# Seven-product down projections in both MLPs of a two-block model, with two pairs of output tiles interleaved

## The chip, the cores and the metric

One core of one Trainium2 chip runs the whole program in one launch. The metric is the device time of an execution in microseconds (us). TensorE multiplies matrices (PE in the profile), VectorE (DVE), ScalarE (ACT) and GpSimd (POOL) do the elementwise work, and DMA queues move data between HBM and the on-chip memory; SP issues most of the weight loads, ACT's queue the rest. Each engine works through its own list of instructions in a fixed order.

## The reference, cut to what matters

Two transformer-like blocks on one sequence of 1024 tokens with 1024 features. Both end in a large MLP with 4096 hidden features, squared ReLU between the two products; block 2 needs modulation vectors from `w_ada`.

```python
x = x + jnp.square(jax.nn.relu(h2 @ w_ff1[l])) @ w_ff2[l]          # block 1
mod = jax.nn.silu(c.astype(jnp.float32)) @ w_ada + b_ada           # [1, 6 * 1024]
mod_c = jax.nn.silu(c_ctx.astype(jnp.float32)) @ w_ada + b_ada
sh1, sc1, gt1, sh2, sc2, gt2 = [m[:, None] for m in jnp.split(mod, 6, axis=-1)]
...
def mlp(s, shift, scale_m):
    hm = rms_norm_2(s, g_norm2) * (1.0 + scale_m) + shift
    return jnp.square(jax.nn.relu(hm @ w_mlp1)) @ w_mlp2           # block 2
x_new = x_new + gt2 * mlp(x_new, sh2, sc2)
```

## The kernel before, in words

Every float32 product is three matmuls of rounded parts: high by high, high by low and low by high (`product`, L123 to L125). `split` (L92, L94) makes the parts: ACT writes the high one, POOL (or DVE on request) subtracts to get the low one. One matmul takes a 128x128 weight and 512 columns. Activations stay on chip as 128x1024 tiles with features on the partitions, in tiles named A, B, C, DD and S by what they hold at the time.

Both MLPs walk through the 4096 hidden features in eight chunks c0 to c7 of 512. A chunk has a first half, the up projection (192 matmuls, `ff1` in block 1), and a second half, the down projection, whose outputs DVE adds to eight running sums of 128x1024.

In block 1 (`mlp1`, L668) the down projection of a chunk is `ff2`: eight calls of `gemm`, 192 matmuls. In chunks 0 to 3 the modulation is woven in: `mod` and `mod_blocks` treat twelve blocks j of 512 columns of `w_ada`, three per chunk. For one block, DVE multiplies eight 128x512 slices of `w_ada` by a column each and adds them up in `acc` (L766, L768, one chain for `c`, and for j below 4 a second for `c_ctx`), transposes the sum (L773) and reduces it (L774); four small matmuls (L778) bring the result to the partitions and DVE adds the bias (L782). The DVE work stands under `later()`, which lets everything else go first. `acc` is one half of the tile DD2 in turn, and the slices come in two loads of 1 MB into DD0 and DD1. Chunk 5 holds `context_norm` and chunk 6 finishes the running sums.

In block 2 (`mlp2`, L1903) the down projection is already done with seven products instead of eight per 2x2 arrangement: `pair_products` takes a pair of output tiles, forms four sums of weight blocks on DVE (tile `ws`, L1849 to L1852), and multiplies them with seven operands that `combine` (L1886 and `put`) forms out of the squared activations: 168 matmuls a chunk. The products gather in four PSUM banks `aux`, and DVE adds each into its outputs (L1970). A bank is used again by a later product only after it has been added out. There are six `aux` buffers and two `acc`.

The order on each engine is set at build time by the framework's scheduler out of program order, priorities (`high_priority`, `later`) and buffers: a tile with one buffer is written again only when all readers of its former content are done.

Of the kernel before, what the change touches and what calls it, by code (L numbers as in the profile page):

```python
# [14 lines left out]
P = 128  # L15
# [39 lines left out]
class Kernel:  # L55
# [319 lines left out]
    def block1(self):  # L375
# [14 lines left out]
        self.delta_setup()  # L390
# [264 lines left out]
    def ff2(self, wap, xh, xl, acc, first, after=None):  # L655
        nc = self.nc

        def evac(ps, js):
            if first:
                nc.scalar.copy(acc[:, js], ps)  # L660
            else:
                nc.vector.tensor_tensor(acc[:, js], ps, acc[:, js], ALU.add)  # L662
            if after:
                after(js)

        self.gemm(wap, xh, xl, evac)

    def mlp1(self):  # L668
# [4 lines left out]
        for c in range(8):  # L673
            ah, al = [], []
            for m in range(4):
                h = self.t(f"C{m}", [P, S], F32R)
                l = self.t(f"C{4 + m}", [P, S], F32R)
                rq = self.t("DD3", [P, 2, S])
                self.ff1(T["w_ff1"][c * 4 + m], self.x1h, self.x1l, h, l, rq[:, 0, :], rq[:, 1, :], rinv if c == 7 else None)
                ah.append(h)  # L680
                al.append(l)
# [7 lines left out]
            for m in range(8 if c < 7 else 0):  # L689
                if c == 0:  # L690
                    acc[m] = self.t(f"S{m}", [P, S])
                after = None
                if c == 6:
                    if m % 2 == 0:
                        x1p = self.t("DD2", [P, 2, S])
                    x1 = x1p[:, m % 2, :]
                    nc.scalar.dma_start(out=x1, in_=self.x1_d[m])

                    def after(js):
                        nc.vector.tensor_tensor(acc[m][:, js], acc[m][:, js], rinv[:, js], ALU.mult)  # L700
# [27 lines left out]
        self.gemm_halves([T["w_ff2"][7, m] for m in range(8)], ah, al, evac)  # L728
# [23 lines left out]
    def mod_blocks(self, j0, j1):  # L752
        nc, T, sil = self.nc, self.T, self.sil
        for j in range(j0, j1):
            n = 2 if j < 4 else 1
            acc = self.t("DD2", [P, 4, 512])[:, 2 * (j % 2) : 2 * (j % 2) + 2]
            for k in range(0, 8, 4):
                w = self.t(f"DD{k // 4}", [P, 4, 512])
                nc.scalar.dma_start(
                    out=w, in_=T["w_ada"][k * P : (k + 4) * P, j * 512 : (j + 1) * 512].rearrange("(a p) c -> p a c", p=P)  # L760
                )
                for kk, i in ((kk, i) for kk in range(4) for i in range(n)):
# [7 lines left out]
            r = w[:, 2, 0 : 16 * n]  # L770
            with self.later():
                for i in range(n):
                    nc.vector.transpose(w[:, i, :], acc[:, i, :])  # L773
                    nc.vector.tensor_reduce(out=r[:, i * 16 : i * 16 + 16], in_=w[:, i, :].rearrange("p (b r) -> p b r", r=32),  # L774
                                            op=ALU.add, axis=AX.X)
# [35 lines left out]
    def delta_setup(self):  # L811
# [14 lines left out]
        self.st = [small(f"st{d}", [P, 8, 64]) for d in range(2)]  # L826
# [266 lines left out]
    def delta_step(self, item, c, el, oacc, seen):  # L1093
# [10 lines left out]
        tmp = self.t(f"dtmp{d}", [64, 4, 64])  # L1104
# [138 lines left out]
    def context_norm(self):  # L1243
# [12 lines left out]
        for k in range(8):  # L1256
            x = raw[:, k, :]
# [6 lines left out]
    def entry(self):  # L1264
# [43 lines left out]
        self.ab = self.t("ab", [P, 8, 32])  # L1308
# [12 lines left out]
    def context(self):  # L1321
# [5 lines left out]
        self.kc2 = [[self.t(f"kc2{p}{i}", [P, L], F32R) for i in range(2)] for p in range(2)]  # L1327
        self.vc = self.t("vc", [P, 2, P])
# [511 lines left out]
    def pair_products(self, raw, ops, evac):  # L1840
# [5 lines left out]
        s = self.t("ws", [P, 4, 2 * P])  # L1846
        a11, a12, a21, a22 = (raw[:, i] for i in range(4))
        s1, s3, s2, s4 = (s[:, i] for i in range(4))
        nc.vector.tensor_tensor(s1, a21, a22, ALU.add)  # L1849
        nc.vector.tensor_tensor(s3, a11, a21, ALU.subtract)  # L1850
        nc.vector.tensor_tensor(s2, s1, a11, ALU.subtract)
        nc.vector.tensor_tensor(s4, a12, s2, ALU.subtract)  # L1852
        banks = {}
        for i, (w, bank, to) in enumerate((
            (a11, 0, [(0, 0)]), (s1, 1, [(1, 1)]), (a12, 2, [(0, 0)]), (s3, 3, [(1, 1)]),
            (s2, 0, [(0, 1), (1, 0), (1, 1)]), (s4, 1, [(0, 1)]), (a22, 3, [(1, 0)]),
        )):
            if i % 2 == 0:
# [15 lines left out]
            for t in to:  # L1874
                evac(t, ps)

    def combine(self, j, qa, qb, ops, m, half):
# [4 lines left out]
        def put(x, i):  # L1882
            h, l = (o[:, j] for o in ops[i])
            self.split(x, h, l)

        sub = lambda o, a, b: nc.vector.tensor_tensor(o, a, b, ALU.subtract)  # L1886
        if m == 0 and half == 0:
            put(qa[:, 0], 0)
        elif m == 0:
            sub(qa[:, 0], qa[:, 1], qa[:, 0])  # L1890
            put(qa[:, 0], 1)
        elif half == 0:
            put(qb[:, 0], 2)
        else:
            sub(qa[:, 1], qb[:, 1], qa[:, 1])
            put(qa[:, 1], 3)
            sub(qa[:, 0], qb[:, 1], qa[:, 0])
            put(qa[:, 0], 4)
            put(qb[:, 1], 5)
            sub(qb[:, 0], qb[:, 0], qa[:, 0])  # L1900
            put(qb[:, 0], 6)

    def mlp2(self):  # L1903
# [3 lines left out]
        for c in range(8):  # L1907
# [3 lines left out]
            qa = [self.t(f"A{6 + j}", [P, 2, 512]) for j in range(2)]  # L1911
            qb = [None, None]
            if c == 0:
                both = self.t("DD3", [P, 2, 2, 512])
                qb = [both[:, j] for j in range(2)]

            def square(m, ps, i):
                if c and m > 1 and i == 0:
                    qb[m % 2] = self.t("S7", [P, 2, 512])
                q = (qa if m < 2 else qb)[m % 2][:, i]  # L1920
                nc.scalar.activation(q, ps, AF.Relu)
                nc.vector.scalar_tensor_tensor(q, ps, 0.0, q, ALU.max, ALU.mult)  # L1922

            if c == 0:
# [216 lines left out]
```

## Time and profile before

| what | value |
|---|---|
| median of 3 runs | 3639.14 us (3637.15 to 3647.19) |
| the profiled execution | 3637.29 us, span 3635.6 us |
| mean granted TensorE clock | 0.978 of full speed |
| PE busy, PEld busy | 3453.7 us (95%), 2777.6 us (76%) |
| DVE busy | 1970.6 us (54%) |
| ACT busy, POOL busy | 1413.0 us (39%), 1627.1 us (45%) |

The span is the time from the first to the last instruction of the profiled execution; 1.7 us lie around it. A single matmul of 512 columns is shown with about 0.4 us, but matmuls are pipelined, and in an undisturbed stretch one starts every 0.23 us. At half clock one starts every 0.43 us.

### The profile page before, as it was taken

What the parts mean: (1) busy time and instruction counts of PE and PEld (TensorE: products, weight loads), DVE (VectorE), ACT (ScalarE), POOL (GpSimd) and SP (SyncE); (2) the same over time, 40 slices, a digit from 0 to 9 for tenths busy, and PEclk for the clock granted to TensorE, in tenths of its full rate; (3) what the DMA queues carried; (4) which work ended last, traced back from release to release, by engine and by line L of the source; (5) the groups of instructions that cost most, each with busy time, mean ns of one, the idle gap of its engine ahead of it and who ended that gap; (6) DMA issues with size and microseconds to landing.
All of it is one profiled execution on the core that took longest, in us unless ns stands there. A gap on an engine that the chain in (4) does not pass through costs nothing. (4 is left out here: it accounts for less than half of the span.)

```text
span 3635.6 us, 49563 instructions
## 1 busy us (share of the span) xinstructions
PE 3453.7 (95%) x17912; PEld 2777.6 (76%) x17912; DVE 1970.6 (54%) x3117; ACT 1413.0 (39%) x3006; POOL 1627.1 (45%) x1894
## 2 busy tenths in 40 slices
PE   8988999999999999999999899979999999999998
PEld 6766777788878887887777788768777877777777
DVE  5576522233454432256377766868876554454445
ACT  4656444423332222225343434334553453333332
POOL 4544422223443333345144475466212565555555
PEclk9998999999999999999999999989999999999999
DMA  3122222243433321133221202211115411111113
GB/s 117 63 70 83 71 67 80 99 139 107 139 115 117 116 70 55 52 100 102 81 76 59 85 33 73 91 56 42 50 48 175 160 57 47 47 47 47 47 47 110
DMA packets 207221, 294.57 MB, mean 81 GB/s; under 512 B 21248, under 2 KB 153472, under 8 KB 206848
## 3 DMA queue, kind: packets, MB, share of 16 engines
q1 hardware_dynamic: 178176, 220.15, 18.4%
q10 hardware_dynamic: 28800, 71.27, 5.9%
q8 instruction: 141, 2.31, 0.3%
q14 instruction: 104, 0.85, 0.1%
HBM read 237.85 MB, written 53.48 MB: 80 GB/s over the span
## 5 line engine op out<-in xcount | busy, mean ns | idle before, releaser
L94 POOL TENSOR_TENSOR wl<-wraw,wh 128x256 fp32r<-128x256 f32 x861 | 717.5, 849 | 1075.6 <-ACT wh L92 1061.5
L124 PE MATMUL acc<-B,wh 128*128 128x512 f32 x1984 | 786.8, 397 | 0.0
L123 PE MATMUL acc<-A,wh 128*128 128x512 f32 (+1 forms) x1920 | 766.6, 399 | 14.4 <-ACT S L1743 11.0
L125 PE MATMUL acc<-A,wl 128*128 128x512 f32 (+1 forms) x1920 | 761.1, 396 | 0.0
L92 ACT ACTIVATE wh<-wraw 128x256 fp32r<-128x256 f32 x925 | 350.4, 411 | 723.2 <-PE acc L124 340.0
L123 PE MATMUL acc<-C,wh 128*128 128x512 f32 x1152 | 456.7, 397 | 4.9 <-DVE S L662 1.5
L125 PE MATMUL acc<-C,wl 128*128 128x512 f32 x1152 | 452.7, 393 | 0.0
L123 PEld LDWEIGHTS acc<-A,wh 128*128 128x128 f32 (+1 forms) x1920 | 361.6, 188 | 105.8 <-ACT S L1743 13.2
L124 PEld LDWEIGHTS acc<-B,wh 128*128 128x128 f32 x1984 | 373.5, 188 | 85.2 <-issue 0.5
L125 PEld LDWEIGHTS acc<-A,wl 128*128 128x128 f32 (+1 forms) x1920 | 361.4, 188 | 85.4 <-POOL wl L94 0.3
L123 PEld LDWEIGHTS acc<-C,wh 128*128 128x128 f32 x1152 | 216.3, 188 | 58.1 <-issue 4.3
L125 PEld LDWEIGHTS acc<-C,wl 128*128 128x128 f32 x1152 | 216.3, 188 | 50.7 <-issue 0.5
L124 PE MATMUL acc<-C,wh 128*128 128x512 f32 x640 | 250.9, 392 | 0.0
L1970 DVE TENSOR_TENSOR DD<-aux,DD 128x512 f32<-128x512 f32 x272 | 178.2, 683 | 64.0 <-PE aux L1873 56.1
L124 PE MATMUL acc<-S,wh 128*128 128x512 f32 x512 | 202.0, 394 | 0.0
L648 DVE SCALAR_TENSOR_TENSOR DD<-acc,DD 128x512 f32<-128x512 f32 x64 | 44.2, 691 | 264.0 <-ACT DD L647 264.0
L94 POOL TENSOR_TENSOR C<-DD,C 128x512 fp32r<-128x512 f32 x64 | 84.4, 1319 | 168.5 <-ACT C L92 168.5
L123 PE MATMUL acc<-DD,wh 128*128 128x512 f32 (+2 forms) x408 | 151.6, 371 | 1.8 <-DVE S L714 1.8
L125 PE MATMUL acc<-DD,wl 128*128 128x512 f32 (+2 forms) x408 | 151.2, 371 | 0.0
L1106 POOL TENSOR_TENSOR dtmp<-st,g_el 64x256 f32<-64x256 f32 x160 | 115.2, 730 | 80.2 <-DVE st L1107 62.7
L124 PEld LDWEIGHTS acc<-C,wh 128*128 128x128 f32 x640 | 120.2, 188 | 25.5
L1872 PE MATMUL aux<-B,wh 128*128 128x512 f32 x256 | 108.3, 423 | 20.0 <-POOL B L94 20.0
(509 smaller groups left out, 6483.8 us busy)
## 6 DMA issues: line engine op xcount, KB each, us to landing
wraw<-in_w_in SPq DMA_DIRECT2D x336, 128.0 KB, 2.1
wraw<-in_w_ff SPq DMA_DIRECT2D x272, 128.0 KB, 2.1
DD<-in_w_ada ACTq DMA_DIRECT2D x24, 1024.0 KB, 5.2
wraw<-in_w_mlp SPq DMA_DIRECT2D x136, 128.0 KB, 2.1
wq<-in_w_mlp SPq DMA_DIRECT2D x32, 512.0 KB, 3.4
wraw<-in_w_out SPq DMA_DIRECT2D x96, 128.0 KB, 2.3
C<-in_rpb SPq DMA_DIRECT2D x24, 384.0 KB, 3.5
tga_d<-S SPq DMA_DIRECT2D x16, 512.0 KB, 3.3
```

The source lines that it names most:

```text
L92: nc.scalar.activation(h, src, AF.Copy)
L94: e.tensor_tensor(l, src, h.bitcast(F32), ALU.subtract)
L123: nc.tensor.matmul(ps, wh, xh, start=first, stop=False)
L124: nc.tensor.matmul(ps, wh, xl, start=False, stop=False)
L125: nc.tensor.matmul(ps, wl, xh, start=False, stop=last)
L648: nc.vector.scalar_tensor_tensor(q[:, js], ps, 0.0, r[:, js], ALU.max, ALU.mult)
L1106: nc.gpsimd.tensor_tensor(tmp, cur[0:64], ev.unsqueeze(2).to_broadcast([64, 4, 64]), ALU.mult)
L1872: nc.tensor.matmul(ps, h, xl[:, k], start=False, stop=False, skip_group_check=not new)
L1970: nc.vector.tensor_tensor(acc[m][:, js], ps, acc[m][:, js], ALU.add)
```

## The change

1. In chunks 0 to 6 of `mlp1` the down projection goes through `pair_products` with seven-product weights; chunk 7 keeps `gemm_halves`. The operands need the tiles C0 to C7 and DD0 to DD2, and the squares DD3.
2. So the modulation moves out of DD0 to DD2: `acc` becomes the single tile `misc`, and the slices of `w_ada` come in four loads of 512 KB in turn into `kc` and `st` (one buffer each). These tiles are used for other things in block 2.
3. `pair_products` takes two pairs at once: three products of the first pair, three of the second, four of the first, four of the second. The sum s1 has a tile `ws1` of its own with two buffers; the other three sums share `ws`, one buffer.
4. `combine` lets DVE make the low parts of operands 4 and 5 instead of POOL.
5. `context_norm` moves from chunk 5 to the seam between the up and down projection of chunk 7, `delta_setup` into block 2, and the block-1 input x1 that chunk 6 adds is loaded into `kc`, `st` and `misc`.

```diff
 def mlp1(self):
-                self.ff1(T["w_ff1"][c * 4 + m], self.x1h, self.x1l, h, l, rq[:, 0, :], rq[:, 1, :], rinv if c == 7 else None)
...
+        for c in range(7):
+            ops = [(self.t(f"C{2 * i}", [P, 2, 512], F32R), self.t(f"C{2 * i + 1}", [P, 2, 512], F32R)) for i in range(4)]
+            for i in range(3):
+                x = self.t(f"DD{i}", [P, 2, 2, 512], F32R)
...
+                for a in range(2):
+                    self.gemm(T["w_ff1"][c * 4 + 2 * a + j], self.x1h, self.x1l, evac)
...
             if c < 4:
                 self.mod(3 * c, 3 * c + 3)
-            if c == 5:
-                self.context_norm()
...
+                    if c == 6:
+                        xs.append(self.t(("kc", "st", "misc")[m % 3], [P, S]))
+                        nc.scalar.dma_start(out=xs[-1], in_=self.x1_d[m])
...
+                    if c == 0 and seen[t] == 1:
+                        nc.scalar.copy(a, ps)
+                    else:
+                        nc.vector.tensor_tensor(a, ps, a, ALU.add)
+                    if c == 6 and seen[t] == (3 if t == (1, 1) else 2):
+                        nc.vector.tensor_tensor(a, a, rinv[:, lat[t[1]]], ALU.mult)
+                        nc.vector.tensor_tensor(a, a, xs[t[0]][:, lat[t[1]]], ALU.add)
...
+            for p in (0, 2):
+                self.pair_products([T["w_ff2"][c, p], T["w_ff2"][c, p + 1]], ops, [adder(p), adder(p + 1)])
...
+        self.context_norm()
...
 def mod_blocks(self, j0, j1):
-            acc = self.t("DD2", [P, 4, 512])[:, 2 * (j % 2) : 2 * (j % 2) + 2]
-            for k in range(0, 8, 4):
-                w = self.t(f"DD{k // 4}", [P, 4, 512])
+            acc = self.t("misc", [P, 2, 512])
+            for k in range(0, 8, 2):
+                w = self.t(("kc", "st")[k // 2 % 2], [P, 2, 512])
...
-            r = w[:, 2, 0 : 16 * n]
+            r = acc[:, 0, 0 : 16 * n]
...
 def pair_products(self, waps, ops, evacs):
+        for n, (p, i) in enumerate([(p, i) for p in range(2) for i in range(3)] + [(p, i) for p in range(2) for i in range(3, 7)]):
+            a11, a12, a21, a22 = (ws[p][:, k] for k in range(4))
+            if i == 0:
+                first[p] = self.t("ws1", [P, 2 * P], bufs=2)
+                nc.vector.tensor_tensor(first[p], a21, a22, ALU.add)
+            s1 = first[p]
+            if i == 3:
+                s = rest[p] = self.t("ws", [P, 3, 2 * P])
+                nc.vector.tensor_tensor(s[:, 2], s1, a11, ALU.subtract)
+                nc.vector.tensor_tensor(s[:, 0], a12, s[:, 2], ALU.subtract)
+                nc.vector.tensor_tensor(s[:, 1], a11, a21, ALU.subtract)
+            s4, s3, s2 = (rest[p][:, k] for k in range(3)) if i >= 3 else (None,) * 3
+            w, bank, to = (
+                (a11, 0, [(0, 0)]), (s1, 1, [(1, 1)]), (a12, 2, [(0, 0)]), (s4, 1, [(0, 1)]), (s3, 3, [(1, 1)]),
+                (s2, 0, [(0, 1), (1, 0), (1, 1)]), (a22, 3, [(1, 0)]),
+            )[i]
...
 def combine(self, j, q, ops, done):
+            put(q[0, 1], 4, "vector")
+            put(q[0, 0], 5, "vector")
```

How the order moves, at three places. First PE in chunk 1 of `mlp1`. Before, the three groups of modulation matmuls (L778) stand apart: one at the end of the up projection and the next some fifty rows into the down projection, here. The names of the rows are output<-activation,weight; C and wh, wl belong to the down projection, DD1 holds the reduced sums.

```order
L124 MATMUL acc_1492_8381<-C7_1457_8165,wh_1487_8357 128x512
L125 MATMUL acc_1492_8381<-C3_1456_8164,wl_1488_8358 128x512
L123 MATMUL acc_1497_8405<-C0_1417_7921,wh_1493_8395 128x512
L778 MATMUL aux_1476_8292<-DD1_1475_8284,id32_1348_7511 32x4 x4
L124 MATMUL acc_1497_8405<-C4_1418_7922,wh_1493_8395 128x512
L125 MATMUL acc_1497_8405<-C0_1417_7921,wl_1494_8396 128x512
```

Now the same three groups (now L791, reading `misc`) stand back to back between the last matmul of the up projection (L125) and the first of the seven products (L1898):

```order
L123 MATMUL acc_1479_8264<-A7_1269_7043,wh_1474_8225 128x512
L124 MATMUL acc_1479_8264<-B7_1270_7044,wh_1474_8225 128x512
L125 MATMUL acc_1479_8264<-A7_1269_7043,wl_1475_8226 128x512
L791 MATMUL aux_1485_8331<-misc_1480_8302,id32_1344_7503 32x8 x4
L791 MATMUL aux_1491_8357<-misc_1486_8338,id32_1344_7503 32x4 x4
L791 MATMUL aux_1497_8382<-misc_1492_8363,id32_1344_7503 32x4 x4
L1898 MATMUL aux_1503_8398<-C0_1427_7957,wh_1501_8394 128x512
```

The second and third group moved ahead of the whole down projection of their chunk. In the changed kernel the rows of chunks 0, 2 and 3 read the same way.

Second, DVE at the same place of the changed kernel: the rest of the middle block (`misc_1486`) and the third block (`misc_1492`), up to its bias (L795). `kc` and `st` hold slices of `w_ada`.

```order
L780 SCALAR_TENSOR_TENSOR misc_1486_8338<-st_1490_8351,sil_1342_7498,misc_1486_8338 128x512 x2
L785 STREAM_TRANSPOSE st_1490_8351<-misc_1486_8338 128x512
L787 TENSOR_REDUCE misc_1486_8338<-st_1490_8351 128x16
L795 TENSOR_TENSOR modc_1343_7502<-aux_1491_8357,cols_1_63 128x4
L778 TENSOR_SCALAR misc_1492_8363<-kc_1493_8364,sil_1342_7498 128x512
L780 SCALAR_TENSOR_TENSOR misc_1492_8363<-kc_1493_8364,sil_1342_7498,misc_1492_8363 128x512
L780 SCALAR_TENSOR_TENSOR misc_1492_8363<-st_1494_8368,sil_1342_7498,misc_1492_8363 128x512 x2
L780 SCALAR_TENSOR_TENSOR misc_1492_8363<-kc_1495_8372,sil_1342_7498,misc_1492_8363 128x512 x2
L780 SCALAR_TENSOR_TENSOR misc_1492_8363<-st_1496_8376,sil_1342_7498,misc_1492_8363 128x512 x2
L785 STREAM_TRANSPOSE st_1496_8376<-misc_1492_8363 128x512
L787 TENSOR_REDUCE misc_1492_8363<-st_1496_8376 128x16
L795 TENSOR_TENSOR modc_1343_7502<-aux_1497_8382,cols_1_63 128x4
```

Before, such rows alternated with the additions of the down projection (L662), and the blocks had two halves of DD2 in turn; now block follows block, the first row of the next (L778) behind the bias row of the last (L795), and no addition of the down projection (L698) stands among them.

Third, DVE in the down projection of chunk 4, in the middle of a group of two pairs; `ws_2016` holds the sums for the next group's first pair, `S1<-aux_1991` adds out the bank that the first pair's last product (a22) writes next.

```order
L1878 TENSOR_TENSOR ws_1994_11390<-wq_1973_11271,ws_1994_11390 128x256
L1873 TENSOR_TENSOR ws1_2002_11441<-wq_2000_11437 128x256
L698 TENSOR_TENSOR S0_1363_7613<-aux_1978_11289,S0_1363_7613 128x512
L1877 TENSOR_TENSOR ws_2016_11511<-ws1_2002_11441,wq_2000_11437 128x256
L1879 TENSOR_TENSOR ws_2016_11511<-wq_2000_11437 128x256
L698 TENSOR_TENSOR S1_1364_7614<-aux_1991_11360,S1_1364_7614 128x512
L1878 TENSOR_TENSOR ws_2016_11511<-wq_2000_11437,ws_2016_11511 128x256
L698 TENSOR_TENSOR S0_1363_7613<-aux_1977_11279,S0_1363_7613 128x512
L698 TENSOR_TENSOR S1_1364_7614<-aux_1977_11279,S1_1364_7614 128x512 x2
```

The sums for the next group (L1877, L1879) come ahead of that addition. Before, in block 2, a pair's four sums were formed together in front of its products.

## Rows read from the trace of the kernel before

**Rows 1.** The page: span, and busy time (share) of each engine

```profile
span 3635.6 us, 49563 instructions
...
PE 3453.7 (95%) x17912; PEld 2777.6 (76%) x17912; DVE 1970.6 (54%) x3117; ACT 1413.0 (39%) x3006; POOL 1627.1 (45%) x1894
```

**Rows 2.** Windows: chunks 0 to 6 of `mlp1`, one row each

```profile
core 0: us, PE busy (x) PEld busy (x) DVE busy (x) ACT busy (x) POOL busy (x), PEclk, DMA share, GB/s
940.10:1036.30 96.20, 93.86 (x429) 74.86 (x428) 70.55 (x102) 30.48 (x67) 41.29 (x40) 1.00 0.43 141
1036.30:1126.60 90.30, 89.91 (x410) 72.45 (x409) 42.56 (x66) 21.48 (x50) 35.87 (x40) 1.00 0.39 129
1126.60:1216.40 89.80, 89.72 (x409) 72.46 (x408) 38.67 (x57) 20.99 (x48) 35.73 (x40) 1.00 0.36 118
1216.40:1306.30 89.90, 89.85 (x409) 72.44 (x408) 32.87 (x45) 22.80 (x49) 34.32 (x40) 1.00 0.26 82
1306.30:1394.90 88.60, 88.60 (x386) 72.22 (x385) 16.60 (x24) 21.00 (x48) 33.30 (x40) 1.00 0.16 48
1394.90:1486.10 91.20, 89.69 (x391) 72.95 (x390) 23.86 (x42) 25.85 (x58) 33.62 (x40) 1.00 0.19 58
1486.10:1574.70 88.60, 88.60 (x385) 72.22 (x385) 40.33 (x54) 20.99 (x48) 36.13 (x40) 1.00 0.25 84
```

**Rows 3.** Windows: the eight down projections of `mlp2`, first, last, sum

```profile
2948.10:2994.80 46.70, 40.85 (x169) 32.22 (x167) 29.85 (x42) 22.94 (x51) 30.50 (x35) 0.93 0.16 57
...
3583.60:3629.80 46.20, 41.70 (x168) 33.15 (x167) 40.94 (x64) 11.31 (x27) 26.85 (x29) 0.93 0.51 176
sum 367.80, PE 330.45 PEld 262.45 DVE 271.96 ACT 113.82 POOL 227.36; mean PE 41.31 PEld 32.81 DVE 33.99 ACT 14.23 POOL 28.42
```

**Rows 4.** PE's timeline in chunk 5 of `mlp2` (start, duration), then a window

```profile
3408.52 0.49 PE L1871 MATMUL aux<-B,wh 128*128 128x512 f32 x1 [1.65 <-ACT B L92]
3411.86 0.79 PE L1872 MATMUL aux<-B,wh 128*128 128x512 f32 x1 [2.85 <-POOL B L94]
...
3412.00:3418.00 6.00, 6.00 (x14) 4.65 (x15) 2.58 (x4) 0.85 (x3) 4.37 (x5) 0.50 0.02 3
```

**Rows 5.** DVE's timeline ahead of those waits

```profile
3403.93 0.94 DVE L1849 TENSOR_TENSOR ws<-wq 128x256 f32<-128x256 f32 x1 [3.48 <-POOL wl L94]
3404.79 0.41 DVE L1850 TENSOR_TENSOR ws<-wq 128x256 f32<-128x256 f32 x1
...
3407.12 2.37 DVE L1886 TENSOR_TENSOR A<-S,A 128x512 f32<-128x512 f32 x2
```

**Rows 6.** PE's timeline at the seam of chunk 0 of `mlp1`

```profile
985.07 0.40 PE L125 MATMUL acc<-A,wl 128*128 128x512 f32 x1
985.31 0.95 PE L183 MATMUL aux<-ones,S 128*128 128x1 f32 x8
...
993.04 0.25 PE L778 MATMUL aux<-DD,id 128*32 128x8 f32 x8
```

**Rows 7.** DVE's timeline there

```profile
993.75 0.22 DVE L782 TENSOR_TENSOR modc<-aux,cols 128x4 f32<-128x4 f32 x2
998.26 2.08 DVE L768 SCALAR_TENSOR_TENSOR DD<-DD,sil,DD 128x512 f32<-128x512 f32 x3 [4.29 <-DMA DD<-in_w_ada]
```

**Rows 8.** DVE's groups, 940 to 1320 us: busy, mean ns, idle before

```profile
L773 DVE STREAM_TRANSPOSE DD<-DD 128x512 f32<-128x512 f32 x16 | 10.9, 696 | 0.1
L774 DVE TENSOR_REDUCE DD<-DD 128x16 f32<-128x512 f32 x16 | 10.5, 673 | 0.3
L766 DVE TENSOR_SCALAR DD<-DD,sil 128x512 f32<-128x512 f32 x16 | 8.9, 565 | 0.2 <-DMA DD<-in_w_ada 0.2
```

**Rows 9.** The page's DMA issues: KB each, us from issue to landing

```profile
DD<-in_w_ada ACTq DMA_DIRECT2D x24, 1024.0 KB, 5.2
...
wq<-in_w_mlp SPq DMA_DIRECT2D x32, 512.0 KB, 3.4
```

**Rows 10.** DVE's and POOL's groups in one down projection of `mlp2`, 3401.8 to 3448.8

```profile
L1970 DVE TENSOR_TENSOR DD<-aux,DD 128x512 f32<-128x512 f32 x35 | 23.0, 684 | 9.4 <-PE aux L1873 9.3
L94 POOL TENSOR_TENSOR wl<-ws,wh 128x256 fp32r<-128x256 f32 x14 | 10.2, 739 | 4.7 <-ACT wh L92 4.7
L94 POOL TENSOR_TENSOR B<-A,B 128x512 fp32r<-128x512 f32 x2 | 3.0, 1524 | 0.0
```

**Rows 11.** PE's timeline early in the kernel

```profile
46.80 3.75 PE L196 MATMUL aux<-S,ones 128*128 128x512 f32 x4 [3.42 <-DVE S L189]
```

More of the change, by code (lines that the diff above doesn't have):

```diff
@@ L653, in ff1_evac @@
         return evac
[L655 to L666, printed above, removed]
     def mlp1(self):
@@ L726, in evac @@
                 self.entry_norm = self.norm_entry(acc, s1[:, js], s2[:, js], js)
[L728 removed]
+        self.gemm_halves([T["w_ff2_last"][m] for m in range(8)], ah, al, evac)
     def mod(self, j0, j1):
@@ L1838, in merge, with pair_products @@
         self.gemm_halves([T["w_out_2"][m] for m in range(8)], mh, ml, evac)
-    def pair_products(self, raw, ops, evac):
+    def pair_products(self, waps, ops, evacs):
         nc = self.nc
[L1846 to L1858, printed above, removed]
+        ws, banks = [], [{}, {}]
+        for wap in waps:
+            raw = self.t("wq", [P, 4, 2 * P], bufs=2)
+            nc.sync.dma_start(out=raw, in_=wap)
+            ws.append(raw)
+        first, rest = [None, None], [None, None]
+        for n, (p, i) in enumerate([(p, i) for p in range(2) for i in range(3)] + [(p, i) for p in range(2) for i in range(3, 7)]):
[14 more added lines that the diff above has]
+            )[i]
+            if n % 2 == 0:
@@ L1868, in pair_products @@
+            ps = banks[p][bank]
             xh, xl = ops[i]
@@ L1910, in mlp2 @@
                 ops.append((self.t(h, [P, 2, 512], F32R), self.t(l, [P, 2, 512], F32R)))
-            qa = [self.t(f"A{6 + j}", [P, 2, 512]) for j in range(2)]
-            qb = [None, None]
             if c == 0:
+                q = [{}, {}]
                 both = self.t("DD3", [P, 2, 2, 512])
[L1915 to L1924, printed above, removed]
+                for j in range(2):
+                    qa = self.t(f"A{6 + j}", [P, 2, 512])
+                    q[j] = {(a, i): (both[:, j] if a else qa)[:, i] for a in range(2) for i in range(2)}
+                done = [[], []]
                 ws = []
@@ L1970, in evac @@
                         nc.vector.tensor_tensor(acc[m][:, js], ps, acc[m][:, js], ALU.add)
-                    if c == 7 and seen[t] == {(0, 0): 2, (0, 1): 2, (1, 0): 2, (1, 1): 3}[t]:
+                    if c == 7 and seen[t] == (3 if t == (1, 1) else 2):
                         x = xs[t[0]][:, js]
@@ L1980, in block2 @@
         self.yd_d = self.d("yd_d", [4, P, S])
+        self.misc = self.t("misc", [P, S])
         self.entry()
+        self.delta_setup()
         self.context()
@@ L2023, in colv @@
     return np.asarray(v).reshape(-1, P).T
-def chunked(w):
-    return np.ascontiguousarray(np.stack([tw(w[c * 512 : (c + 1) * 512]) for c in range(8)]))
 def paired(w):
```

155 lines of the change are left out of this document (82 added, 73 removed).

## The prediction

> **What bounds the kernel now.** First the page: PE is busy 95% of the span and every other engine about half [rows 1], so time is PE's time, and what counts is how many matmuls there are and where PE waits. Then windows by stage. In `mlp1` an undisturbed chunk takes 88.6 us (c4 and c6 in [rows 2]); the program issues 384 matmuls in it, so one costs 88.6 / 384 = 0.231 us, at granted clock 1.00. Against 88.6, chunks 0 to 3 and 5 lose 7.6, 1.7, 1.2, 1.3 and 2.6 us: the modulation costs PE almost nothing there, although DVE works 33 to 71 us in these chunks, because PE has the down projection's matmuls while DVE works.
>
> In `mlp2` the reader sees the opposite. The eight down projections take 367.8 us [rows 3]; 8 x 168 matmuls at 0.231 are 310.1, so 57.7 us are lost, 7.2 each. PE's timeline shows one of them [rows 4]: two waits of 1.65 and 2.85 us for the late operands 5 to 7, and then 14 matmuls in 6 us at granted clock 0.50, the 1.2 GHz level. That slow stretch costs 6.0 - 14 x 0.231 = 2.8 us, as much as a wait. Ahead of the waits, DVE stood 3.48 us for POOL before it could write `ws`, with the operands' subtractions behind it in the queue [rows 5].
>
> **The change, part by part** (against the profiled execution, 3637.3 us).
>
> (a) Fewer matmuls: 7 chunks x 24 x 0.231 = **-38.8**.
>
> (b) The modulation in chunks 0 to 3. `misc` is one buffer: block j+1 can start on DVE only when block j's matmuls have read it, and PE's order puts all three groups of a chunk ahead of the first product. The first block of a chunk is ready early (in chunk 0 it is computed at the start of the kernel); for the second and third PE has nothing else and stands for DVE, ACT's loads and the round trip. One block with a single vector (j from 4 on), from rows: a multiplication 0.57 [rows 8], seven accumulations at 2.08 / 3 = 0.69 [rows 7], a transpose 0.70 and a reduction 0.67 [rows 8]; then the matmuls to the bias row, 993.04 to 993.97, 0.9 [rows 6, 7]. Together 7.7 us. Besides, the slices come through two single buffers: a load of 512 KB takes 3.4 us [rows 9] and can start only when the earlier slices in that buffer are used up, while each half gives DVE only 2 x 0.69 of work, so the third and fourth load add about 3 us and the next block's first load about as much again. I walked through chunk 1 row by row. From the last up-projection matmul: 1.2 us to the first multiplication of the middle block; its next operations are mixed with the last squares, subtractions and low parts, 7.0; its third and fourth slice arrive at 11.3 and 12.0, so its bias row comes at 16.3; the third block's fourth slice, whose load waits until the second is used up at 20.3, lands at 23.7, and its bias comes at 26.8. First product at 27.5. Then PE comes back cold: 14 slow matmuls, 2.7 [rows 4], and about 0.5 for DVE being late. So 30.7 in place of the 1.4 lost now, **+29.3** for each of chunks 1 to 3, +88. Bounds: with all loads hidden 2 x 7.7 + 5 for the mixed rows, 20; with loads as slow as the 1 MB ones, 5.2 [rows 9], four of them in the chain, 35.
>
> Chunk 0 has two vectors, so 2 x 0.57 + 14 x 0.69 + 2 x 0.70 + 2 x 0.67 + 0.9 = 14.4 a block, and 15 to 16 with loads (a half now gives 4 x 0.69 of work). The statistics at this seam (L183 to L778) now run with PE idle as well, 985.3 to 993.0, 7.7 us [rows 6]. 7.7 + 1 for the bias + 2 x 15.6 + 2 for the operands' rows on DVE = 42, and 3 for the cold restart and late sums: 45 in place of 7.6, **+37.4**.
>
> (c) The down projections of chunks 4 and 5. In a group of two pairs DVE has 18 additions at 0.684 [rows 10] and eight weight sums at 0.41 [rows 5], 15.6 us against 14 x 6 x 0.231 = 19.4 of PE: it fits. But DVE's order puts the next group's sums ahead of the addition that the first pair's last product waits for. `ws` is one buffer, and POOL has read the second pair's sums only at about 13.7 us (some ten low parts at 0.74 [rows 10], after the late 512-column ones at 1.5); DVE finishes that addition at 14.5 to 15.2, and PE wants its bank at 12.5. A wait of 2.5 in the first group, none in the second; I add 1.0 for the clock, which falls in some chunks. 2 x 3.5, less the 2.6 of the context norm that leaves chunk 5: **+4.4**.
>
> (d) Chunk 6. DVE is busy 40.3 us there now [rows 2], of which the 32 closing operations are half. Added are 20 additions, 13.7, 16 weight sums, 6.6, and ten subtractions and low parts of the operands, 6.8: 67.4, of which some 57 fall into the down projection, against 38.8 of PE. The banks come free at DVE's pace. Some 4.5 us of additions at the end run beside chunk 7's up projection; **+13.5** stay (10 to 18).
>
> (e) Chunk 7 with the context norm, and `delta_setup` in block 2: the norm's DVE rows lie beside matmuls as before. If that cover is gone the price is the 2.6 of chunk 5. I take **+1**.
>
> (f) `mlp2`. Interleaving moves the late operands behind six products in place of three, and DVE makes two low parts that POOL took 1.5 us each for [rows 10]. The waits of [rows 4] go. Next late is the addition of (c). Six chunks at 3.4, chunk 0 at 1.6, and chunk 7, where DVE works 40.9 us already [rows 3], at 5: 27 in place of 57.7, **-31**. Bounds: -58 if nothing waits, -10 if 4.5 us and the clock are lost in each.
>
> (g) The first modulation block, some 15 us of DVE work, now lies in the first 100 us. One accumulation comes between the rows of the statistics for which PE waits 3.42 us [rows 11]. **+2** (0 to 5).
>
> Sum: -38.8 + 37.4 + 88 + 4.4 + 13.5 + 1 - 31 + 2 = +76.5, so 3713.8 by the profiled execution, which lies 1.9 below the median; I say **3714**.
>
> **A rule weighed.** The added weight sums and low parts read two tiles from SBUF each. The rows show such an operation at 0.41 alone and at 0.94 when it came right behind POOL's, and two 512-column subtractions at 2.37 [rows 5] where twice 0.684 [rows 10] is 1.37. The Trainium skill, SBUF — State Buffer, section "SBUF: two separate sides", says that a DVE operation with two SBUF inputs and a GpSimd operation that reads SBUF exclude each other for the whole instruction. By that rule every such DVE row can cost up to one POOL operation more; the rows agree for some and not for others. The sum by the one is 3714; by the other it is the third rival's.
>
> **The rivals.**
>
> 1. *The modulation is hidden, as the change would need it* (other side). The place is the seam of chunks 0 to 3; it decides whether PE has products to run while blocks two and three are computed. For it: nothing depends on these blocks until block 2. Against it: PE runs its list in order, and the groups stand in front. Without (b)'s 125: 3637.3 - 49 = 3588.
>
> 2. *Shorter waits.* Loads hidden in the chains, 20 in place of 27.5 (-22), chunk 0 5 shorter, `mlp2` back to -50 (-19), chunk 6 at 10 (-3.5): 3664. For it: the loads' engine is little used in `mlp1`, a share of 0.16 to 0.43 [rows 2]. Against it: one buffer per slice pair.
>
> 3. *DVE and POOL collide.* Each of the 12 steady down projections loses 2 to 3 us more, as the excess of 0.53 and 1.00 of these rows would make of four or five collisions: +24 to 36, 3738 to 3750. For it: [rows 5]. Against it: most additions read PSUM and one tile, and hold 0.684 on average beside a busy POOL [rows 10].
>
> 4. *Cold engine.* After waits of 15 to 30 us PE stays at half clock longer than 14 matmuls, say twice as long, at ten places: +27, 3741. For it: a much longer idle than any seen. Against it: in [rows 4] one stretch followed two waits.
>
> **How the numbers follow.** Forecast (3690 to 3732 by the middle bounds of b to f) 0.62; rival 1 0.05; rival 2 0.13; rivals 3 and 4 together 0.15; what I don't see 0.05, mostly below. 0.3% is 11 us, about what a measurement tells from no change. Faster: rival 1 and half of the unseen, 0.08; within: 0.03; slower 0.89. The range leaves out rival 1, the unseen and the far ends of 2 and 3: 3660 to 3748.
>
> **What would show it.** Right: 168-matmul down projections, and in chunks 1 to 3 a gap on PE of 25 to 30 us, 40 in chunk 0, whose waits name DVE `misc` or the modulation matmuls (L791), with DVE waiting for `w_ada` inside; granted clock 0.5 after each; chunk 6 with PE waiting for DVE's additions; `mlp2` down projections of 41 to 43 us. Wrong: PE gaps under 15 us at these seams, which fells (b); `mlp2` at 46 as now, which fells (f); or half clock lasting well over 6 us, which is rival 4.

## The result, and the profile after

The changed kernel is slower: a median of 3762.24 us (3758.04 to 3762.99, 4 runs) against 3639.81 us, a ratio of 1.0331 with a 95% interval of 1.0315 to 1.0348. The direction and the largest cause were forecast; the size was not: +122 us in place of +76.5.

The windows of chunks 0 to 6 of `mlp1` in the changed kernel answer to [rows 2]; the columns are the same.

```profile
944.00:1074.10 130.10, 93.20 (x405) 73.76 (x404) 79.12 (x129) 39.16 (x86) 48.23 (x54) 0.83 0.27 85
1074.10:1192.20 118.10, 86.94 (x385) 69.25 (x384) 71.07 (x109) 29.07 (x67) 47.83 (x54) 0.87 0.28 90
1192.20:1307.70 115.50, 86.33 (x385) 68.80 (x384) 70.06 (x106) 29.02 (x66) 47.88 (x54) 0.88 0.29 91
1307.70:1423.40 115.70, 87.68 (x386) 70.03 (x385) 63.87 (x98) 29.04 (x67) 45.92 (x54) 0.87 0.23 78
1423.40:1513.30 89.90, 86.54 (x362) 69.48 (x361) 48.19 (x74) 28.81 (x67) 46.58 (x54) 0.96 0.15 47
1513.30:1600.30 87.00, 83.64 (x362) 67.56 (x361) 47.47 (x74) 28.79 (x66) 47.16 (x54) 1.00 0.14 49
1600.30:1704.60 104.30, 90.60 (x361) 70.67 (x360) 65.58 (x100) 28.35 (x66) 47.78 (x54) 0.92 0.20 65
sum 760.60, PE 614.92 PEld 489.54 DVE 445.35 ACT 212.24 POOL 331.39; mean PE 87.85 PEld 69.93 DVE 63.62 ACT 30.32 POOL 47.34
```

With 24 matmuls less, a chunk could take 83.1 us. None does: the seven took 634.6 us before (940.1 to 1574.7) and take 760.6 now. PE's waits from 985 to 1424 us (engine, line waited for, sum, times, longest) name the reason for the first four:

```profile
PE aux L791 <- DVE misc L787: 113.4, 8, 16.2
PE aux L1898 <- DVE S L698: 6.2, 5, 1.6
PE aux L196 <- DVE S L189: 5.6, 2, 4.2
```

Eight waits, two per chunk: the modulation's second and third block. DVE's timeline of the seam of chunk 1 shows one such chain from its bias to the next:

```profile
1135.76 0.16 DVE L795 TENSOR_TENSOR modc<-aux,cols 128x4 f32<-128x4 f32 x1 [0.41 <-PE aux L791]
1135.85 0.49 DVE L778 TENSOR_SCALAR misc<-kc,sil 128x512 f32<-128x512 f32 x1
...
1139.28 1.54 DVE L780 SCALAR_TENSOR_TENSOR misc<-st,sil,misc 128x512 f32<-128x512 f32 x2 [2.16 <-DMA st<-in_w_ada]
1141.84 1.54 DVE L780 SCALAR_TENSOR_TENSOR misc<-kc,sil,misc 128x512 f32<-128x512 f32 x2 [1.02 <-DMA kc<-in_w_ada]
1144.64 1.54 DVE L780 SCALAR_TENSOR_TENSOR misc<-st,sil,misc 128x512 f32<-128x512 f32 x2 [1.26 <-DMA st<-in_w_ada]
...
1148.05 0.16 DVE L795 TENSOR_TENSOR modc<-aux,cols 128x4 f32<-128x4 f32 x1 [0.41 <-PE aux L791]
```

12.3 us for one block, of which 4.4 are waits for loads. The down projections of `mlp2` answer to [rows 3]; here the first two, the last and the sum:

```profile
3086.70:3132.10 45.40, 41.20 (x169) 32.26 (x167) 29.02 (x45) 22.45 (x51) 27.08 (x32) 0.96 0.17 59
3177.00:3220.90 43.90, 40.74 (x168) 32.37 (x167) 35.16 (x56) 12.91 (x33) 24.52 (x30) 0.96 0.18 61
...
3709.70:3754.50 44.80, 41.42 (x168) 32.26 (x167) 40.28 (x65) 10.86 (x27) 21.29 (x24) 0.96 0.53 173
sum 353.80, PE 327.29 PEld 259.14 DVE 280.72 ACT 110.75 POOL 195.62; mean PE 40.91 PEld 32.39 DVE 35.09 ACT 13.84 POOL 24.45
```

14.0 us less than before, not 31. In each of the six between the first and the last, one wait of 3.1 to 3.2 us stays, for the addition that frees a22's bank, and with it a stretch of slow clock. The first one is another case: PE still waits there for late operands, ACT's high part and POOL's low part of `A`. The last waits 1.8 us for additions and 1.4 for a weight's high part. Here are the first one's waits:

```profile
PE aux L1898 <- ACT A L92: 1.9, 1, 1.9
PE aux L1899 <- POOL A L94: 1.5, 1, 1.5
```

DVE's and PE's timeline of the second, and two of POOL's rows from the same stretch:

```profile
3179.19 2.38 DVE L1913 TENSOR_TENSOR A<-A,A 128x512 f32<-128x512 f32 x2
3181.49 0.68 DVE L1994 TENSOR_TENSOR DD<-aux,DD 128x512 f32<-128x512 f32 x1
3182.09 1.82 DVE L94 TENSOR_TENSOR B<-A,B 128x512 fp32r<-128x512 f32 x2
...
3190.32 0.93 DVE L1877 TENSOR_TENSOR ws<-ws,wq 128x256 f32<-128x256 f32 x1 [0.71 <-POOL wl L94]
3191.17 0.94 DVE L1879 TENSOR_TENSOR ws<-wq 128x256 f32<-128x256 f32 x1
3192.03 0.68 DVE L1994 TENSOR_TENSOR DD<-aux,DD 128x512 f32<-128x512 f32 x1
3192.86 0.47 PE L1898 MATMUL aux<-B,wh 128*128 128x512 f32 x1 [3.16 <-DVE DD L1994]
...
3179.32 1.70 POOL L94 TENSOR_TENSOR B<-A,B 128x512 fp32r<-128x512 f32 x1 [0.35 <-ACT B L92]
3190.24 1.58 POOL L94 TENSOR_TENSOR wl<-wq,wh 128x256 fp32r<-128x256 f32 x2
```

The addition at 3192.03 stands behind two sums for the next group (L1877, L1879), as the order said. DVE hardly rests before it.

The balance between the two traces, in the steps of the prediction: start of `mlp1` 944.0 against 940.1, +3.9; chunks 0 to 6, +126.0; chunk 7 to the start of block 2's long products (1704.6 to 1843.8 against 1574.7 to 1704.3), +9.6; block 2 up to the first down projection of `mlp2` -0.9; from there to the end -13.6. Together 125.0, the difference of the spans.

### The profile page after: what moved, and what is told of

It reads as the page before. It is cut to its first block, busy times and chain, and to the rows that moved or that the text cites. A ratio compares the mean times of both kernels' runs of the same rounds, so it can differ in the third digit from the quotient of the medians.

```text
span 3760.6 us, 49645 instructions
## 1 busy us (share of the span) xinstructions
PE 3443.8 (92%) x17744; PEld 2760.7 (73%) x17744; DVE 2191.1 (58%) x3485; ACT 1466.3 (39%) x3134; POOL 1662.0 (44%) x1960
## 5 line engine op out<-in xcount | busy, mean ns | idle before, releaser
L94 POOL TENSOR_TENSOR wl<-wraw,wh 128x256 fp32r<-128x256 f32 x749 | 625.2, 850 | 898.1 <-ACT wh L92 880.9
L125 PE MATMUL acc<-A,wl 128*128 128x512 f32 (+1 forms) x1920 | 761.6, 397 | 0.0
L92 ACT ACTIVATE wh<-wraw 128x256 fp32r<-128x256 f32 x813 | 308.1, 410 | 525.8 <-PE acc L124 188.4
L125 PEld LDWEIGHTS acc<-A,wl 128*128 128x128 f32 (+1 forms) x1920 | 361.5, 188 | 85.8 <-POOL wl L94 0.4
L94 POOL TENSOR_TENSOR wl<-ws,wh 128x256 fp32r<-128x256 f32 x240 | 192.4, 812 | 282.1 <-ACT wh L92 279.8
L123 PE MATMUL acc<-C,wh 128*128 128x512 f32 x704 | 281.0, 399 | 6.8 <-DVE S L726 5.8
L125 PE MATMUL acc<-C,wl 128*128 128x512 f32 x704 | 278.3, 395 | 0.0
L92 ACT ACTIVATE wh<-ws 128x256 fp32r<-128x256 f32 x240 | 94.4, 412 | 331.2 <-PE aux L1899 194.5
L698 DVE TENSOR_TENSOR S<-aux,S 128x512 f32<-128x512 f32 x236 | 153.6, 681 | 34.7 <-PE aux L1900 33.5
L94 POOL TENSOR_TENSOR wl<-wq,wh 128x256 fp32r<-128x256 f32 x180 | 140.1, 786 | 52.5 <-ACT wh L92 52.1
L123 PEld LDWEIGHTS acc<-C,wh 128*128 128x128 f32 x704 | 132.5, 188 | 41.8 <-issue 9.7
L125 PEld LDWEIGHTS acc<-C,wl 128*128 128x128 f32 x704 | 132.6, 188 | 32.3 <-issue 0.5
L125 PE MATMUL acc<-DD,wl 128*128 128x512 f32 (+2 forms) x408 | 151.2, 371 | 0.0
```

Source lines behind the costliest of these rows:

```text
L92: nc.scalar.activation(h, src, AF.Copy)
L94: e.tensor_tensor(l, src, h.bitcast(F32), ALU.subtract)
L123: nc.tensor.matmul(ps, wh, xh, start=first, stop=False)
L125: nc.tensor.matmul(ps, wl, xh, start=False, stop=last)
L698: nc.vector.tensor_tensor(a, ps, a, ALU.add)
```

## The experiments

Each is the changed kernel with one edit, unless it is said otherwise, and its median is compared with the changed kernel's 3762.24. The kernel before, measured again beside each of the three groups of runs, gave 3640.33, 3641.63 and 3639.84 us, within 2 us of the 3639.81 above. Two theories of the seams (the places between the up and the down projection of a chunk) were open. Theory A is the prediction's: the single SBUF buffer `misc`. Theory B is the order of the PSUM buffers: in the kernel before, the down projection's products used the PSUM buffers `acc`, and the modulation's `aux`; now both use `aux`.

**Another PSUM buffer for the modulation** (e1).

```diff
-            ps = self.p("aux", [P, 512], AUX)
+            ps = self.p("acc", [P, 512], ACC)
...
```

> The result of the modulation matmuls goes to a PSUM buffer acc instead of aux; nothing else changes. Theory A (single SBUF buffer misc makes PE wait, as the prediction says): the groups are as late as before, 3755 to 3765 us. Theory B (the six aux buffers are handed out in program order, so the first product has to wait until all three modulation groups of its chunk have had theirs): the order on PE now has the groups inside and at the end of the down projection; the middle chain is hidden, the third, which starts only when misc is free, stands at the chunk's end with 10 to 13 us. Seams of 29 become about 13 in chunks 1 to 3 and 43 becomes 10 to 20 in chunk 0: 3675 to 3695 us.

3710.36 us, 52 less. This one tag moves the groups on PE from the seam into the down projection. The same waits from 985 to 1424 us:

```profile
PE acc L791 <- DVE misc L787: 37.8, 4, 12.0
PE aux L1898 <- DVE S L698: 19.3, 9, 3.0
PE aux L196 <- DVE S L189: 6.6, 2, 4.8
```

113.4 became 37.8, four waits in place of eight: theory A alone falls. The four that stay are the third blocks, at the end of each chunk, as expected of the single buffer. The gain is less than the 67 to 87 that theory B expected. In part that is because the additions now share DVE with the chains: PE's waits for them went from 6.2 to 19.3.

**A second SBUF buffer for every second block from block 4 on, PSUM as it was** (e2).

```diff
-            acc = self.t("misc", [P, 2, 512])
+            acc = self.t("misc", [P, 2, 512]) if n == 2 or j % 2 == 0 else self.t("macc", [P, 1, 512])
```

> From block 4 on, every second modulation block adds up in a second SBUF buffer; PSUM stays aux. Theory A: the third chain of chunks 1 to 3 no longer waits for the second's matmuls and the seams shrink by 5 to 10 us each, 3735 to 3748 us. Theory B: PE still has all three groups ahead of its products, and DVE makes one chain after the other anyway, so only the round trip of about 1 us a chain goes: 3755 to 3762 us.

3744.14 us, 18 less. That is within the range of theory A (3735 to 3748) and misses that of theory B (3755 to 3762). PE waits in the same window:

```profile
PE aux L791 <- DVE misc L787: 62.7, 4, 16.9
PE aux L791 <- DVE macc L787: 27.9, 2, 14.9
```

Six waits in place of eight. In chunks 2 and 3 two blocks now were ready at the seam and one chain stood; the order of PE's rows did not change. So neither theory holds alone: the PSUM turns decide where the chains stand, and the number of SBUF buffers decides how many. Both are needed for the 113. The waits for loads inside a chain (4.4 us in the block above) were not tested by a run with more buffers for the slices.

**PSUM `acc`, and two blocks a chunk in chunks 0 to 5** (e3).

```diff
-            if c < 4:
-                self.mod(3 * c, 3 * c + 3)
+            if c < 6:
+                self.mod(2 * c, 2 * c + 2)
...
```

> As the first run (PSUM acc), and two modulation blocks in each of chunks 0 to 5 in place of three in chunks 0 to 3. Theory B with misc as the second cause: one block is ready at the seam and the other is made beside 39 us of products, so no chain stands before PE: about 125 us less than the changed kernel, 3630 to 3650 us. Theory A: one chain of 13 to 15 us stays in each of six chunks, 3720 to 3735 us.

3678.24 us, 84 less, and 28 above the range of theory B. Of the modulation's waits one of 7.6 us is left, but PE's waits for additions (L698) up to 1424 us are 23.2: the chains now run in DVE's fullest stage, and the additions that free the banks come late.

**Chain and matmuls of a block written apart** (e9): eight blocks beside `mix`, whose two last loops hold sixteen `gemm`s, four in chunks 0 to 3, one per seam.

```diff
+            if m % 2 == 0:
+                self.mod_chain(m // 2)
             self.mix_tile(T["w_rec_o"][m], rh, rl, self.tgr_d[m], a1[m], h, l, m)
+            if m % 2:
+                self.mod_turn(m // 2)
...
```

> Chain and matmuls of a modulation block are written apart: eight blocks run beside mix, the last four one per seam, each chain a whole stage ahead of its matmuls; everything else as in the changed kernel. Theory B with one buffer as second cause: no seam of chunks 0 to 3 stands any more except the statistics of chunk 0 (8 to 12 us); chunks 0 to 3 take 87 to 92 us as chunks 4 and 5 do: 3632 to 3648 us, so no faster than the kernel before, since the wait for the bank, chunk 6 and chunk 7 give back what 168 matmuls save. Rival (the DVE work of the modulation costs wherever it stands): 3655 to 3680 us.

3663.07 us, 99 less, and still 1.0063 (1.0048 to 1.0078) of the kernel before: the modulation no longer stands before PE, and the change is still no gain. It is 15 us above the expected range and inside the rival's, that the modulation's DVE work costs wherever it stands. The seams of chunks 1 to 3 are gone, and that of chunk 0 is 12 us, its statistics. Chunks 0 to 3 still take 101, 93, 92 and 88 us, with 18.2 us of waits for additions up to 1424 us, and some 4 us are lost between the start of `mix` and chunk 0.

**The weight sums as tiles of their own in five buffers** (e4).

```diff
-                s = rest[p] = self.t("ws", [P, 3, 2 * P])
+                s2, s4, s3 = (self.t("ws", [P, 2 * P], bufs=5) for _ in range(3))
...
```

> The three weight sums are tiles of their own in five buffers instead of one tile in one buffer. Theory W (DVE waits for POOL to read the second pair's sums, then adds out the bank that the first pair's last product wants): the wait of 3.5 us per steady down projection falls below 1.5, and most half-clock stretches with it: 45 us less, 3710 to 3720 us. Theory L (DVE is behind by its own load in the first group: operands, sums, contention with POOL; the wait for POOL is only 0.7 us in the trace): 1 us less in each of 14 down projections, 3742 to 3755 us.

3749.19 us, 13 less, as theory L said. The six middle down projections of `mlp2` take 41.3 to 44.3 us in place of 43.9; the second has a wait of 2.0 for the same addition, the fourth one of 3.4. The down projections of chunks 0 and 2 of `mlp1` are 2 to 3 us longer. The sums can now be written earlier and wait for POOL elsewhere:

```profile
3172.35 0.98 DVE L1880 TENSOR_TENSOR ws<-wq 128x256 f32<-128x256 f32 x1 [5.29 <-POOL wl L94]
3173.25 0.68 DVE L1931 SCALAR_TENSOR_TENSOR A<-acc,A 128x512 f32<-128x512 f32 x1
```

**Low parts 4 and 5 back on POOL** (e5).

```diff
-            put(q[0, 1], 4, "vector")
-            put(q[0, 0], 5, "vector")
+            put(q[0, 1], 4)
+            put(q[0, 0], 5)
```

> The low parts of operands 4 and 5 go back from DVE to POOL (part 4 of the change undone). Theory L (DVE is behind by its own load in the first group of a down projection): 1.8 us of DVE work goes from in front of the additions, the wait before a22 shrinks by 1 to 1.8 us in each of 14 down projections: 3735 to 3750 us. Rival (the operands come late by POOL, as in the kernel before, where it took 1.5 us for each): a new wait of 1 to 3 us for operands 5 to 7, 3770 to 3800 us.

3782.22 us, 20 more, where theory L said a gain. The rival has the sign and the range, but not the place: PE still waits for the addition, 3.9 to 4.5 us in place of 3.2, and for no operand; the six middle down projections take 45.0 to 46.3 us. The trace shows another delay. POOL makes the two low parts first (3190.95 to 3194.19) and reads the weights in `wq` behind them; the next load into `wq`, which waits for that, is issued at 3195.10, and DVE stands for it before it can form the next sum:

```profile
3198.52 0.42 DVE L1873 TENSOR_TENSOR ws<-wq 128x256 f32<-128x256 f32 x1 [2.56 <-DMA wq<-in_w_mlp]
```

In the changed kernel DVE stands 0.3 us for this load. So the edit takes work off DVE and brings a delay of its own, and the run does not decide on theory L. Part 4 of the change is worth its place.

**The last product of both pairs at the end of the group** (e6).

```diff
-        for n, (p, i) in enumerate([(p, i) for p in range(2) for i in range(3)] + [(p, i) for p in range(2) for i in range(3, 7)]):
+        for n, (p, i) in enumerate([(p, i) for p in range(2) for i in range(3)] + [(p, i) for p in range(2) for i in range(3, 6)] + [(0, 6), (1, 6)]):
```

> The last product a22 of both pairs stands at the end of the group; the order on DVE now has the addition that frees its bank ahead of the next group's sums. Theory K (the steady loss of 4 to 7 us per down projection is that one wait for the bank plus the half-clock stretch behind it): 14 down projections lose 0.5 to 1.5 us instead, 3700 to 3715 us. Theory L in its strong form (DVE is the bound of the group): the wait moves to the next bank, less than 1 us each is won, 3748 to 3762 us.

3724.33 us, 38 less. Windows of this kernel: two down projections of `mlp2`, the last one, and chunk 4 of `mlp1`:

```profile
3159.80:3199.40 39.60, 39.11 (x168) 31.39 (x167) 31.81 (x55) 12.96 (x33) 23.91 (x30) 1.00 0.20 67
3244.30:3283.80 39.50, 39.01 (x168) 31.35 (x167) 32.15 (x54) 12.90 (x33) 24.24 (x30) 1.00 0.19 68
3666.40:3715.30 48.90, 41.54 (x169) 32.50 (x167) 39.34 (x64) 10.89 (x27) 21.74 (x24) 0.93 0.46 158
1463.30:1502.60 39.30, 38.65 (x169) 31.26 (x168) 32.78 (x54) 12.79 (x33) 24.12 (x30) 1.00 0.20 69
```

43.9 became 39.6, near the 38.8 of the matmuls alone, at clock 1.00, with DVE 3.4 us less busy (31.8 in place of 35.2). So in a steady down projection DVE's load is not the bound; it is the one wait and the slow clock behind it. The order also took away long rows on DVE (the sum of L1877 takes 0.46 us on average in place of 0.86), and the run does not tell the two apart. The gain is below the expected 47 to 62: the last chunk is 4.1 us longer than in the changed kernel, and the first down projection of `mlp2`, where PE waits for operands, gains only 0.4.

**The closing operations of chunk 6 at the lowest priority** (e7).

```diff
+                        with self.later():
-                        nc.vector.tensor_tensor(a, a, rinv[:, lat[t[1]]], ALU.mult)
-                        nc.vector.tensor_tensor(a, a, xs[t[0]][:, lat[t[1]]], ALU.add)
+                            nc.vector.tensor_tensor(a, a, rinv[:, lat[t[1]]], ALU.mult)
+                            nc.vector.tensor_tensor(a, a, xs[t[0]][:, lat[t[1]]], ALU.add)
```

> The 32 closing operations of chunk 6 get the lowest priority. Theory (DVE's load in chunk 6, 21 us over the ideal there, is these operations between the additions): they move beside chunk 7's up projection, chunk 6 loses 6 to 9 us instead of 21, and nothing is given back later: 3745 to 3752 us. Rival: they delay the squares of chunk 7, the context norm and the additions behind it, 3757 to 3765 us.

3754.07 us, 8 less (3752.48 to 3755.51, against 3758.04 to 3762.99). Chunk 6's down projection and chunk 7's up projection in this kernel:

```profile
1641.70:1685.20 43.50, 39.67 (x171) 31.46 (x170) 41.68 (x66) 13.20 (x34) 27.69 (x30) 1.00 0.24 76
1685.20:1735.00 49.80, 46.38 (x193) 36.93 (x191) 30.32 (x43) 15.39 (x32) 26.36 (x20) 0.97 0.33 103
```

In the changed kernel they take 59.7 and 44.6. Chunk 6 gains 16.2, and PE's waits for ACT's high parts are gone from it. In chunk 7's up projection, where DVE has 9 us more to do, 5.2 come back; where the rest of the difference to 8 goes was not told apart. Theory and rival both hold in part.

**The context norm ahead of chunk 7's up projection** (e8).

```diff
+        self.context_norm()
         ah, al = [], []
...
-        self.context_norm()
...
```

> The context norm comes ahead of chunk 7's up projection, its input in DD2. Theory (its DVE operations at the seam of chunk 7 delay the additions of the last down projection, 8 us later than in the kernel before): 6 to 8 us less, 3753 to 3757 us. Rival (chunk 7's loss is the late end of chunk 6): no change, 3760 to 3764 us.

3761.71 us: no change. The down projection of chunk 7 starts 1749.2 in the changed kernel and 1754.0 here, and block 2's long products at 1843.8 and 1840.4: the loss moves into the up projection and what comes behind. PE's waits for additions in chunk 7's down projection (1754 to 1841 us) are back at what they are in the kernel before:

```profile
PE acc L123 <- DVE S L726: 5.1, 3, 2.2
```

They are 9.8 in the changed kernel. So the norm's rows account for 4.7 us there, and cost about as much (49.4 us in place of 44.6) in the up projection. What the rest of the 9.6 us is was not told apart.

**The parts of `mlp2` alone, in the kernel before** (e11), and **the same with a22 at the end of the group in chunks 0 to 6** (e12).

> The kernel before with the change in mlp2 alone (interleaved pairs, ws1, low parts 4 and 5 on DVE). The trace of the changed kernel says 13.6 us less than before: 3624 to 3630 us. The prediction said 31 less: 3606 to 3612 us.

> The same with a22 at the end of the group in chunks 0 to 6 of mlp2. Theory K: down projections of 39.6 us in six chunks: 38 to 42 us less than before, 3597 to 3604 us. Rival (block 2 alone can't give that, since it showed so in a kernel with other timing): 3620 to 3630 us.

3624.43 us, 0.9960 (0.9945 to 0.9975), and 3596.58 us, 0.9878 (0.9862 to 0.9895): 15 and 43 us less than the kernel before, the first as the trace of the changed kernel said, the second 0.4 us below the range of theory K. The second is the fastest kernel here and beats both. Two of its down projections, a steady one and the last:

```profile
3124.60:3164.20 39.60, 39.11 (x169) 31.40 (x168) 31.86 (x56) 12.95 (x33) 23.90 (x30) 1.00 0.19 68
3547.00:3592.10 45.10, 41.83 (x168) 32.05 (x167) 40.32 (x65) 10.99 (x27) 20.35 (x24) 0.96 0.51 171
```

**Everything together** (e10): e9, a22 at the end of the group (not in the last chunk of `mlp2`), and e7 with the closing additions on POOL.

> The same, with a22 at the end of the group (but not in the last chunk of mlp2) and the closing operations of chunk 6 at the lowest priority, their second half on POOL. If the causes add up (125 for the modulation, 38 and 4 for the bank, 8 to 14 for chunk 6): 3575 to 3595 us, faster than both kernels. If they share a cover: 3600 to 3630 us.

3603.43 us, 0.9896 (0.9882 to 0.9911): faster than both kernels, above the sum of the causes and no better than e12. In `mlp1` the seven products pay only where DVE has room. Chunks 3 to 5 take 84.2 to 84.3 us in place of 88.6 to 91.2; chunks 0 and 6 take 97.0 and 89.7, no less than before (96.2 and 88.6). Here are chunks 0, 4 and 6:

```profile
948.90:1045.90 97.00, 91.41 (x392) 72.87 (x389) 53.30 (x85) 38.49 (x86) 48.99 (x54) 0.95 0.28 91
...
1308.50:1392.70 84.20, 83.55 (x362) 67.67 (x361) 46.26 (x74) 28.93 (x67) 46.77 (x54) 1.00 0.16 50
...
1476.90:1566.60 89.70, 84.68 (x361) 68.01 (x360) 52.19 (x76) 28.18 (x64) 60.91 (x61) 0.99 0.19 63
```

The seven chunks take 617.7 us, 17 less than in the kernel before; chunk 7 to block 2's long products takes 14 more than before (1566.6 to 1710.2), and `mlp1` starts 8.8 later. So what `mlp1` gains in its chunks it loses around them.

## Why the prediction was wrong in size

The two traces differ by 125.0 us, 48.5 more than the sum of 76.5. (a) held, and so did the direction. (b), the modulation, was sized nearly right: PE stood 43.0 us at the seam of chunk 0 (988.4 to 1031.4; 42 said) and 29.0, 28.4 and 28.9 in chunks 1 to 3 (27.5 said). Its cause was half right: e1 and e2 show that the single `misc` buffer makes the chains follow each other, and that the turns of the PSUM buffer `aux` put them ahead of the products. Reading only the wait, the prediction did not ask why PE's order had changed. Chunks 0 to 3 lose 2.0, 4.3, 1.7 and 1.9 us more than said. About half of these 9.9 lies in the seams; the other half goes with PE's waits for late additions, 6.2 us, for which the sum allowed 0.5 a chunk.

The step that failed is what it said of DVE's late addition and of DVE's load: terms (f), (c), (d) and (e). They make 37 of the 48.5.

- (f): -13.6 in place of -31, the largest miss.
  - In the six middle chunks the mechanism was right and its size wrong: each loses 5.1 us where 3.4 was said. The wait is 3.2 us in place of 2.5, and it brings the slow clock in every chunk (0.96 in each window), some 1.9 us of it, where the sum put 1.0 for a clock that falls in some.
  - Ahead of that wait, DVE's rows are long where they run beside POOL's: 2.38 for two subtractions, 1.82 for two low parts, 0.93 and 0.94 for sums of 0.41, some 2.5 us more than alone. The rule of the Trainium skill, SBUF — State Buffer, section "SBUF: two separate sides", agrees with these rows: they have two SBUF inputs, and the additions, which take one input from PSUM, keep 0.68. That would be rival 3 at about half the price that it named; that these rows alone make the wait longer is read from the rows, and no run separates it.
  - In the first chunk the mechanism was wrong: "The waits of [rows 4] go" does not hold there, PE waits 1.9 and 1.5 us for operands, and 6.6 us are lost where 1.6 was said.
  - e6 shows that the wait for a22's bank, with the slow clock behind it, is nearly the whole of the loss in the six middle chunks (39.5 to 39.6 us with it gone, against 38.8), and not in the first, which takes 45.0 us there too.
- (c): chunks 4 and 5 take 89.9 and 87.0, where 86.6 each was said. Both have one wait of 3.4 us for the addition, in place of 2.5; the slow clock follows it in chunk 4 (0.96) and not in chunk 5 (1.00).
- (d): chunk 6 takes 104.3, 21.2 over the ideal in place of 13.5. The sum had the banks come free at DVE's pace, and PE's waits for additions are 3.6 us. Its larger waits, 10.0, are of a kind that the sum left out. With DVE full, the weight sums are late too, and through ACT's high part the matmuls themselves. The last line is ACT's wait for those sums between 1654 and 1705 us:

```profile
1666.05 0.79 PE L1898 MATMUL aux<-C,wh 128*128 128x512 f32 x1 [3.91 <-ACT wh L92]
...
1695.54 0.79 PE L1898 MATMUL aux<-C,wh 128*128 128x512 f32 x1 [6.08 <-ACT wh L92]
...
ACT wh L92 <- DVE ws L1878: 29.1, 2, 16.8
```

The slow clock (0.86 in the down projection) goes with them. e7 shows that DVE's closing operations are the main cause: with them out of the way the stage takes 43.5 us at clock 1.00.

- (e): +9.6 in place of +1. "The norm's DVE rows lie beside matmuls as before" was false for chunk 7: PE's waits for additions (L726) from 1749 to 1844 are 9.8 us against 5.1 in the same stage before, and e8 shows that the norm's rows make this difference. The other half of the miss stays open.
- (g): +3.9 in place of +2, within its bounds, but by luck: PE waits 5.92 us for DVE's sum of squares (L237) up to 43.48 us, earlier than the row that was named, and the modulation's first multiplication (L778) starts at 43.42, behind that sum. Why the sum is later than before is open.

These misses have one sign. (c), (e) and (f) took DVE as free when its sum of work fitted; (d) took it as full, and none priced that in such a stage DVE, ACT and POOL hand work to each other, so that one being late makes the next late. Rival 1 was wrong for the kernel as it stands; e9 has the modulation hidden, and would have been 3588 by rival 1's sum, not 3663, so that sum was 75 us too good. Rival 2 fell: the seams did not shrink to 20 us, the loads stood in the chains, and `mlp2` gained 14 and not 50. Rival 4 fell: behind the four seams 6 to 14 matmuls were slow, no more than the 14 of [rows 4].

## What to carry to other kernels

When a stage takes over a buffer tag, ask whose turns in it come earlier in program order: a small side calculation in the same PSUM tag can stop all matmuls behind it, and another tag took away two thirds of the waits here. In a chain of products that reuse banks, put the product that reuses a bank last (here worth 4.3 us in each steady stage), and look at what stands ahead of its freeing addition in the adding engine's order. An engine that is half idle over the span can be the bound of the stage that gets more of its work: price it there, together with the engines that feed it.

## What the runs showed of the hardware

The slow stretch behind a wait did not grow with the wait. After 12.0 us of waiting at the seam of chunk 1, and 16.2 just before, the granted clock was 0.50, the 1.2 GHz level, for the next 4 us, and 1.00 from there:

```profile
1147.50:1151.50 4.00, 3.80 (x17) 3.01 (x17) 2.08 (x6) 0.00 (x0) 0.00 (x0) 0.50 0.54 145
1152.00:1158.00 6.00, 6.00 (x28) 4.97 (x27) 5.01 (x10) 1.45 (x4) 3.29 (x4) 1.00 0.41 148
```

Behind the seams of chunks 0, 2 and 3, where PE stood 28 to 43 us but for the small matmuls of the modulation and the statistics, matmuls started 0.43 us apart for 4.7, 2.7 and 6.1 us. In the middle chunks of `mlp2`, behind waits of 3.1 to 3.2 us, they did so for 3.5 to 3.7. Two equal waits of 3.4 us, in chunks 4 and 5 of `mlp1`, were followed by 6.0 us of it and by none.
